# Two projections of a hybrid decoder: value columns taken 512 at a time, and where the deferred pieces stand

## The chip, the cores and the metric

The kernel runs on one core of a Trainium2 chip. The metric is the device time of one launch in microseconds, the median of the runs. TensorE (PE in the profile) multiplies, VectorE (DVE), ScalarE (ACT) and GpSimd (POOL) do the elementwise work, and SyncE (SP) and ScalarE issue the transfers. Each engine works through its own queue in order.

## What is computed

Two layers, 512 tokens, width 1024, 256 memory tokens, all float32. Each layer projects the normed residual to 6664 columns, feeds four groups of heads, multiplies each group by its gate and maps back with one output projection:

```python
def hybrid_layer(x, mem, ...):
    proj = rmsnorm(x, pre_g) @ w_in
    y_ret = retention(ret_q, ret_k, ret_v) * silu(ret_g)          # 4 heads of 128, decay masks
    y_ssd = ssd_mixer(xbc, z, dt_raw, ...)                        # conv, chunked scan, 8 heads of 64
    y_sb = stick_breaking(sb_q, sb_k, sb_v) * silu(sb_g)          # 4 heads of 128
    y_mem = memory_read(mem_q, rmsnorm(mem), w_mem_kv) * silu(mem_g)
    y = concatenate([y_ret, y_ssd, y_sb, y_mem]) @ w_out
    return x + rmsnorm(y, post_g)

def memory_read(q, mem_n, w_mem_kv):
    k, v = split(mem_n @ w_mem_kv, 2)                             # 256 tokens x 512 each
    return softmax(q @ k.T * d ** -0.5) @ v
```

Retention normalises each head's output over its 128 features. The kernel takes the mean out of the values, sums the squares over the features with a matmul against ones, and multiplies the output by the reciprocal root of each token.

## The kernel before

Every operand of a matmul is split into a high part h and a low part l, both float32r, and a product is three matmuls, h h + h l + l h (`mm3`). The residual lies turned, features first, in `hTh` and `hTl`, eight chunks of 128 features (kc).

**Projections.** `proj_b` gives 128 output features for all 512 tokens: the weights are the stationary side, hT the moving one, 8 x 3 matmuls of 512 columns. It is used for queries, keys, gates and the convolution's inputs. `proj_a` gives values with the tokens on the partitions: a slice of hT of 128 tokens is stationary and 256 columns of weights move. It takes the feature chunks in two halves of four, and in each half goes over the token chunks (four, two for the memory). So 512 value columns need two calls; two token chunks share a bank of 512 columns. The stick-breaking values (`sb_v`) call it with 8 columns more for dt, and once without. The retention values (`ret_v`) call it twice, the memory values (`mem_v`) once for each half of the columns.

**Weights.** They come from memory in blocks of 1 MB (`raw`, two buffers), each cut in two half-blocks. A half-block of 128 x 1024 is split by one cast on ScalarE (L286, to `wh`) and one subtraction on VectorE (L287, to `wl`). There are five buffers of wh and wl; `w_take` hands out the next half-block, and `w_prefetch` writes the splits that follow, five half-blocks ahead. A split waits until the buffer's earlier matmuls are over.

**Values.** `ret_v` subtracts each head's mean (reduction L681, scaling L686) and splits the result into pairs. `mem_v2` scales by the memory's norm and splits.

**Order.** The program counts units: each `proj_b` is one (`tick`), each `proj_a` two. Work that has to wait is put off with `defer(n, f)` and runs n units later. For a retention head, `ret_head2` multiplies scores by values and squares them on two half-partitions (L743, L744, L746, L747), `ret_head3` runs a one-row matmul of ones and those squares (`onesr`), and `row_rstd` makes the reciprocal root: a copy of the row (L707), a DMA to 32 partitions (L709), GpSimd's add and power (L710, L711), a DMA to memory (L713) and one that broadcasts it to 128 partitions (L715). `scaled` (L757) multiplies the head's output by it, five units after. Each retention head is three units: q, k and a gate of the memory group. After the heads come the two SSD groups, with convolution (L808, L810, L813) and gates (L821, L953).

The framework's scheduler sets the final order of each engine's queue, from the dependences and its own estimate of times; the start (`start`) alone is written out by hand. Tiles come from pools: `s` (33 buffers of 512 columns), `y` (16), `r` (9), and eight PSUM banks, four `pj` for projections and four `mx` for the rest.

Of the kernel before, what the change touches and what calls it, by code (L numbers as in the profile page):

```python
# [78 lines left out]
def pack_weights(w_in, w_mem_kv, w_out):  # L79

    src = {"w_in": w_in, "w_mem_kv": w_mem_kv, "w_out": w_out}
    out = []
    for l in range(DEPTH):
        for kind, name, spec in BLOCKS:
            w = src[name][l]
            o = []
            for s in range(2):
                if kind == "b":
                    t = w[:, spec[s]:spec[s] + P].reshape(KC, P, P)
                elif kind == "o":  # L90
                    half, j = spec
                    rows = OUT_ROWS[4 * j + 2 * s:4 * j + 2 * s + 2]
                    t = np.stack([w[r:r + P, 512 * half:512 * half + 512] for r in rows])
                elif kind == "d":
# [73 lines left out]
class Builder:  # L168
# [206 lines left out]
    def proj_a(self, x=None, nt=NT, extra=0, between=(), turns=False):  # L375
# [3 lines left out]
        xh, xl = x or self.hk  # L379
        n = 256 + extra  # L380
# [3 lines left out]
        for s in range(2):  # L384
            for f in between if s else ():
                f()
            w = [self.w_take(nk) for _ in range(4 // nk)]
            if self.starting:
                (wh, wl), out = w[0], banks[0]
                for low in range(2):  # L390
                    for t in range(nt):
                        for j in range(4):
                            o, kc, ts = out[:, n * t:n * t + n], 4 * s + j, slice(P * t, P * t + P)
                            first, last = s + low + t + j == 0, (s, low, t, j) == (1, 1, nt - 1, 3)
                            if low:
                                self.mm(o, xh(kc)[:, ts], wl[:, j], False, last)
                            else:
                                self.mm(o, xh(kc)[:, ts], wh[:, j], first, False)
                                self.mm(o, xl(kc)[:, ts], wh[:, j], False, False)
                continue  # L400
# [8 lines left out]
            self.w_prefetch()  # L409
        return banks  # L410
# [130 lines left out]
    def mem_v(self):  # L541
        self.mem_v2(self.proj_a(self.mx_, 2)[0])

    def mem_v2(self, b):
        nc, p = self.nc, Pair(self, 512, "y")
        for t in range(2):
            s, r = slice(256 * t, 256 * t + 256), self.mcol[:, t:t + 1]
            nc.scalar.activation(p.h[:, s], b[:, s], AF.Copy, scale=r)
            nc.vector.scalar_tensor_tensor(out=p.l[:, s], in0=b[:, s], scalar=r, in1=p.hf[:, s], op0=ALU.mult, op1=ALU.subtract)
        self.mv.append(p)  # L550
# [78 lines left out]
    def sb_head(self, h, v):  # L629
# [3 lines left out]
        w = [t[:, c] for t, c in self.packed([P * (t + 1) for t in range(NT)], self.buf)]  # L633
# [18 lines left out]
        self.defer(3, self.sb_head2, h, v, w, y)  # L652
        return y

    def sb_head2(self, h, v, w, y):
# [7 lines left out]
        self.defer(1, self.sb_head3, h, v, wT, y)  # L663
# [9 lines left out]
    def ret_v(self):  # L673
# [3 lines left out]
        out = [[None, None], [None, None]]  # L677
        for half in range(2):
            for i, b in enumerate(self.proj_a()):
                st = self.tiny(4)  # L680
                nc.vector.tensor_reduce(out=st, in_=v3(b, 4), op=ALU.add, axis=AX.X)  # L681
                nc.vector.tensor_scalar(out=st, in0=st, scalar1=-1.0 / HD, scalar2=None, op0=ALU.mult)
                vt = self.buf()
                for j in range(4):
                    t, h = 2 * i + j // 2, 2 * half + j % 2
                    nc.vector.tensor_scalar(out=vt[:, P * j:P * j + P], in0=b[:, P * j:P * j + P],  # L686
                                            scalar1=st[:, j:j + 1], scalar2=ginv[:, 4 * t + h:4 * t + h + 1],
                                            op0=ALU.add, op1=ALU.mult)
                out[i][half] = self.pair(vt)
# [45 lines left out]
    def ret_head2(self, h, v, sc, y):  # L735
        nc = self.nc
        b = self.mx()
        for c in range(NT):
            self.mm3(b[:, P * c:], *self.vcols(v, c, h), sc[c][0], sc[c][1], c == 0, c == NT - 1)
# [10 lines left out]
    def ret_head3(self, h, z, y):  # L750
# [219 lines left out]
    def out_proj(self, l):  # L970
# [51 lines left out]
        if not last:  # L1022
# [3 lines left out]
            for i in range(2):  # L1026
                self.mem_v()
            self.behind(self.turn[2], self.marks[1])
# [43 lines left out]
    def start(self):  # L1072
# [37 lines left out]
        def v0():  # L1110
            a.append(self.normed_a(xs[2]))
            self.turned(hn[0], 0)
        v = [self.proj_a(self.mx_, 2, between=[v0])[0]]
        self.w_prefetch(7)
        hn.append(self.normed_b(a[2], preB))
        self.turned(hn[1], 1)
        a.append(self.normed_a(xs[3]))
        self.mem_cols()
        self.w_prefetch(8)
        hn.append(self.normed_b(a[3], preB))  # L1120

        def v1():
            self.turned(hn[2], 2)
        v.append(self.proj_a(self.mx_, 2, between=[v1])[0])
# [5 lines left out]
        for i in range(2):  # L1130
            self.mem_v2(v[i])
# [8 lines left out]
    def layer(self, l):  # L1140
        self.exp_ln_phase()
        while len(self.mv) < 2:
            self.mem_v()
# [54 lines left out]
```

## Time and profile before

| | us |
|---|---|
| median of 3 runs (961.93 to 963.8) | 961.94 |
| profiled execution | 961.89 |
| its span | 960.2 |
| TensorE busy | 949.8 |
| VectorE busy | 657.4 |
| ScalarE busy | 456.8 |
| GpSimd busy | 104.4 |

The span is what the trace covers; 1.7 us of the profiled execution lie around it. Durations of matmuls overlap (a matmul of 512 columns is shown with some 390 ns, and the next one starts 227 ns after it), so starts are to be compared. "Idle before" is the time in which an engine had nothing in hand ahead of an instruction, with what ended it.

### The profile page before, as it was taken

To read this page: it belongs to the slowest core of one execution; us is meant where nothing else is said; L and a number is where in the kernel's file an instruction comes from. 1 tells how busy PE (TensorE), PEld (TensorE's weight loads), DVE (VectorE), ACT (ScalarE), POOL (GpSimd) and SP (SyncE) were. 2 spreads that over 40 slices of the span, in tenths; PEclk is the share of its full clock that TensorE was granted. 3 is DMA by queue.
4 is the path that set the end of the run, shared out by engine and by line. 5 is a ranking of instruction groups with operands and counts; after the bars stand their busy time and mean duration, and the time that the engine had idled before them with its cause. 6 is when DMAs were issued, how large, how long until landed. Compare 5 with 4: busy or idle time off the path is not lost.

```text
span 960.2 us, 13253 instructions
## 1 busy us (share of the span) xinstructions
PE 949.8 (99%) x5151; PEld 812.6 (85%) x5151; DVE 657.4 (68%) x1056; ACT 456.8 (48%) x844; POOL 104.4 (11%) x160
## 2 busy tenths in 40 slices
PE   9999999999999999999999999999999999999997
PEld 7998889988887888888899888898888878888885
DVE  5855567767777796854487465768777968877443
ACT  6544566534554342643465345665344543435341
POOL 1100000001231201100040000000003421102001
PEclk9999999999999999999999999999999999999999
DMA  9442212122232524344344222112222333423502
GB/s 347 149 147 80 88 45 88 45 88 88 91 108 99 165 88 121 115 160 142 120 170 184 89 88 71 62 45 88 77 78 85 134 105 116 120 91 120 195 25 87
DMA packets 26734, 105.79 MB, mean 110 GB/s; under 512 B 4144, under 2 KB 4400, under 8 KB 17456
## 3 DMA queue, kind: packets, MB, share of 16 engines
q10 hardware_dynamic: 10224, 73.44, 21.8%
q1 hardware_dynamic: 16448, 31.52, 10.0%
q8 instruction: 40, 0.66, 0.3%
q14 instruction: 22, 0.18, 0.1%
HBM read 100.63 MB, written 4.28 MB: 109 GB/s over the span
## 4 chain that ended last, share of the span: by engine, by line
PE 88%; DVE 5%; DMA 3%; ACT 1%; issue 1%; POOL 1%; DVEq 0%; SPq 0%; ACTq 0%; POOLq 0%
PE pj L278 65%; PE mx L278 22%; DVE s L647 1%; DMA r<-row 1%; PE mx L599 1%; PE mx L449 1%; DMA mem<-memT 1%; DMA s<-acs 1%; DVE wl L287 1%; DMA t<-r 1%; POOL t L711 1%; DVE s L810 1%; DVE s L646 0%; PE mx L661 0%; DVE s L287 0%
## 5 line engine op out<-in xcount | busy, mean ns | idle before, releaser
L278 PE MATMUL pj<-hTh,wh 128*128 128x512 f32 x704 | 277.5, 394 | 0.0
L278 PE MATMUL pj<-hTl,wh 128*128 128x512 f32 x704 | 276.6, 393 | 0.0
L278 PE MATMUL pj<-hTh,wl 128*128 128x512 f32 x704 | 275.4, 391 | 0.0
L287 DVE TENSOR_TENSOR wl<-raw,wh 128x1024 fp32r<-128x1024 f32 (+2 forms) x155 | 183.7, 1190 | 114.2 <-ACT wh L286 107.3
L286 ACT CAST wh<-raw 128x1024 fp32r<-128x1024 f32 (+2 forms) x155 | 158.0, 1025 | 178.9 <-PE pj L278 153.7
L278 PEld LDWEIGHTS pj<-hTh,wl 128*128 128x128 f32 x704 | 132.3, 188 | 26.7
L278 PEld LDWEIGHTS pj<-hTh,wh 128*128 128x128 f32 x704 | 132.3, 188 | 26.4
L278 PEld LDWEIGHTS pj<-hTl,wh 128*128 128x128 f32 x704 | 132.4, 188 | 25.7
L278 PE MATMUL pj<-wh,s 128*128 128x512 f32 (+1 forms) x384 | 99.8, 355 | 0.0
L278 PE MATMUL mx<-s,s 128*128 128x256 f32 (+4 forms) x616 | 97.5, 310 | 0.3
L278 PEld LDWEIGHTS mx<-s,s 128*128 128x128 f32 (+1 forms) x616 | 84.6, 178 | 12.9 <-issue 3.1
L278 PE MATMUL mx<-wh,s 128*128 128x512 f32 x256 | 79.2, 389 | 0.0
L278 PEld LDWEIGHTS pj<-wh,s 128*128 128x128 f32 x384 | 66.1, 189 | 10.5
L730 POOL TENSOR_SCALAR_AFFINE_SELECT s<-s 128x128 fp32r<-128x128 f32 x64 | 21.2, 363 | 420.6 <-DVE s L287 420.6
L278 PE MATMUL pj<-wl,s 128*128 128x512 f32 (+1 forms) x192 | 63.4, 354 | 0.0
L278 PE MATMUL pj<-wh,hTh 128*128 128x256 f32 (+1 forms) x208 | 60.3, 290 | 0.5 <-DVE s L556 0.5
L287 DVE TENSOR_TENSOR s<-mx,s 128x512 fp32r<-128x512 f32 (+2 forms) x86 | 42.1, 517 | 26.0 <-ACT s L286 25.6
L278 PE MATMUL pj<-wl,hTh 128*128 128x256 f32 (+1 forms) x208 | 59.5, 286 | 0.0
L278 PE MATMUL pj<-wh,hTl 128*128 128x256 f32 (+1 forms) x208 | 58.5, 284 | 0.0
L278 PEld LDWEIGHTS mx<-wh,s 128*128 128x128 f32 x256 | 48.1, 188 | 10.0
L286 ACT CAST s<-mx 128x512 fp32r<-128x512 f32 (+2 forms) x86 | 36.7, 456 | 40.1 <-PE mx L278 24.1
L287 DVE TENSOR_TENSOR s<-y,s 128x512 fp32r<-128x512 f32 x64 | 41.3, 688 | 19.7 <-ACT s L286 14.0
(167 smaller groups left out, 1324.5 us busy)
## 6 DMA issues: line engine op xcount, KB each, us to landing
raw<-wts ACTq DMA_DIRECT2D x69, 1024.0 KB, 4.8
s<-x SPq DMA_DIRECT2D x24, 256.0 KB, 3.7
s<-acs SPq DMA_DIRECT2D x16, 256.0 KB, 6.1
raw<-wts SPq DMA_DIRECT2D x3, 1024.0 KB, 8.3
r<-row SPq DMA_DIRECT2D x12, 256.0 KB, 3.9
s<-acs SPq DMA_DIRECT2D x16, 128.0 KB, 6.7
x<-s SPq DMA_DIRECT2D x8, 256.0 KB, 2.0
out<-s SPq DMA_DIRECT2D x8, 256.0 KB, 2.0
```

The costliest lines, as they stand in the source:

```text
L278: return self.nc.tensor.matmul(out, lhsT, rhs, start=start, stop=stop)
L286: self.nc.scalar.copy(h, src)
L287: self.nc.vector.tensor_sub(l, src, hf)
L449: x = self.nc.tensor.transpose(b[:, P * j:P * j + P], hn[i][:, P * j:P * j + P], self.con("ident", P))
L599: nc.tensor.transpose(b[:, P * t:P * t + P], w[t // 2][:, o:o + P], self.con("ident", P))
L647: nc.vector.tensor_tensor_scan(out=u[:, ::-1], data0=u[:, ::-1], data1=u[:, ::-1], initial=0.0, op0=ALU.add, op1=ALU.bypass)
L711: nc.gpsimd.tensor_tensor(out=c, in0=c, in1=self.mhalf[:RP], op=ALU.pow)
L730: nc.gpsimd.affine_select(out=d, in_=d, pattern=[[1, P]], compare_op=ALU.is_ge, fill=0.0, base=0, channel_multiplier=-1)
L810: nc.vector.scalar_tensor_tensor(out=acc[:, s:], in0=b[:, :SEQ - s], scalar=tap(3 - s), in1=acc[:, s:], op0=ALU.mult, op1=ALU.add)
```

## The change

The values of the memory and of the retention are projected by a new function, `proj_v`: 512 columns of weights move at once, and one token chunk follows the other, each through all eight feature chunks into a bank of its own. For that the half-blocks are packed anew (kind "v": 256 features by 512 columns), four of them are taken ahead of the first chunk, and the prefetch of the next four is written behind the last. Each token chunk counts one unit for the retention values and two for the memory values. In the start, where the weights still arrive, it goes half-block by half-block instead, over both token chunks. `proj_a` stays for the stick-breaking values.

```diff
-    b += [("a", "w_mem_kv", GW + 256 * i) for i in range(2)]
+    b += [("v", "w_mem_kv", (GW, 512 * i)) for i in range(2)]
...
-    b += [("a", "w_in", RET_V + 256 * i) for i in range(2)]
+    b += [("v", "w_in", (RET_V, 512 * i)) for i in range(2)]
...
+    def proj_v(self, x=None, nt=NT, between={}):
+        xh, xl = x or self.hk
+        banks = [self.pj() for _ in range(nt)]
+        self.marks = []
+        if self.starting:
...
+        w = [self.w_take(2) for _ in range(4)]
+        for t in range(nt):
+            self.tick(4 // nt)
+            ts = slice(P * t, P * t + P)
+            for kc in range(KC):
+                wh, wl = w[kc // 2]
+                self.mm3(banks[t], xh(kc)[:, ts], xl(kc)[:, ts], wh[:, kc % 2], wl[:, kc % 2], kc == 0, kc == KC - 1)
+                if kc % 2:
+                    self.marks.append(self.last_mm)
+        self.w_prefetch()
+        return banks
```

The tiles of values now hold one token chunk and all heads, so their users take other columns of them:

```diff
+        for t, b in enumerate(banks):
+            p, r = Pair(self, 512, "y"), self.mcol[:, t:t + 1]
+            nc.scalar.activation(p.h, b, AF.Copy, scale=r)
+            nc.vector.scalar_tensor_tensor(out=p.l, in0=b, scalar=r, in1=p.hf, op0=ALU.mult, op1=ALU.subtract)
+            self.mv.append(p)
...
-            o = 256 * m + HD * (h % 2)
-            v = self.mv[h // 2]
+            o, v = HD * h, self.mv[m]
...
+        for t, b in enumerate(self.proj_v()):
+            st = self.tiny(HEADS)
+            nc.vector.tensor_reduce(out=st, in_=v3(b, HEADS), op=ALU.add, axis=AX.X)
+            nc.vector.tensor_scalar(out=st, in0=st, scalar1=-1.0 / HD, scalar2=None, op0=ALU.mult)
+            vt = self.buf(tag="r")
+            for h in range(HEADS):
+                c = slice(HD * h, HD * h + HD)
+                nc.vector.tensor_scalar(out=vt[:, c], in0=b[:, c], scalar1=st[:, h:h + 1],
+                                        scalar2=ginv[:, 4 * t + h:4 * t + h + 1], op0=ALU.add, op1=ALU.mult)
+            out.append(self.pair(vt))
```

The deferred pieces get other distances, the weight tiles of the stick-breaking heads another pool, and `scaled` is pinned to its place in the program's order:

```diff
-        w = [t[:, c] for t, c in self.packed([P * (t + 1) for t in range(NT)], self.buf)]
+        w = [t[:, c] for t, c in self.packed([P * (t + 1) for t in range(NT)], lambda: self.buf(tag="r"))]
...
-        self.defer(3, self.sb_head2, h, v, w, y)
+        self.defer(4, self.sb_head2, h, v, w, y)
...
-        self.defer(1, self.sb_head3, h, v, wT, y)
+        self.defer(2, self.sb_head3, h, v, wT, y)
...
-        self.defer(5, self.scaled, y, self.row_rstd(vb, self.con("reps", HEADS * RJ, RP)[:, RJ * h:RJ * h + RJ]))
+        self.defer(7, self.scaled, y, self.row_rstd(vb, self.con("reps", HEADS * RJ, RP)[:, RJ * h:RJ * h + RJ]))
...
-        self.nc.vector.tensor_mul(y, y, rB)
+        self.tc.keep_in_program_order(self.nc.vector.tensor_mul(y, y, rB))
```

Two places of the queues show what moves. The first is VectorE's queue where the first SSD group begins, in layer 0. Before, the scaling of head 2 (L757) stands ahead of the squares of head 3 (L744, L747):

```order
L810 SCALAR_TENSOR_TENSOR s_3113<-pj_3084,hp_776,s_3113 128x510
L810 SCALAR_TENSOR_TENSOR s_3113<-pj_3084,hp_776,s_3113 128x509
L287 TENSOR_TENSOR wl_3147<-raw_2946,wh_3146 128x1024
L757 TENSOR_TENSOR y_2632<-y_2632,r_2915 128x512
L744 TENSOR_TENSOR r_3008<-r_3008,r_3009 64x512
L813 SCALAR_TENSOR_TENSOR s_3114<-s_3114,s_3113 128x512
L810 SCALAR_TENSOR_TENSOR s_3152<-pj_3121,hp_776,s_3152 128x511
L747 TENSOR_TENSOR r_3013<-r_3008,r_3013 64x512
L810 SCALAR_TENSOR_TENSOR s_3152<-pj_3121,hp_776,s_3152 128x510
L810 SCALAR_TENSOR_TENSOR s_3152<-pj_3121,hp_776,s_3152 128x509
```

After, line numbers are 18 or 19 higher there: L762 and L765 are L744 and L747, L776 is L757, L829 and L832 the convolution, L840 and L972 a gate. The first row is the scaling of head 1, the last that of head 2:

```order
L776 TENSOR_TENSOR y_2298<-y_2298,r_2552 128x512
L829 SCALAR_TENSOR_TENSOR s_3004<-pj_2973,hp_724,s_3004 128x511
L765 TENSOR_TENSOR r_2864<-r_2859,r_2864 64x512
L829 SCALAR_TENSOR_TENSOR s_3004<-pj_2973,hp_724,s_3004 128x510
L290 TENSOR_TENSOR wl_3038<-raw_2896,wh_3037 128x1024
L829 SCALAR_TENSOR_TENSOR s_3004<-pj_2973,hp_724,s_3004 128x509
L832 SCALAR_TENSOR_TENSOR s_3005<-s_3005,s_3004 128x512
L840 SCALAR_TENSOR_TENSOR s_3041<-s_3041,pj_3012 128x512
L972 SCALAR_TENSOR_TENSOR y_1449<-y_1449,s_3041 128x512
L290 TENSOR_TENSOR wl_3073<-raw_2896,wh_3072 128x1024
L840 SCALAR_TENSOR_TENSOR s_3078<-s_3078,pj_3047 128x512
L776 TENSOR_TENSOR y_2484<-y_2484,r_2766 128x512
```

Head 3's L765 now has head 1's scaling ahead of it, and head 2's scaling stands behind it, two weight splits and a gate further on.

The second place is VectorE's queue at the end of the retention values of layer 0. Before, the rows around one weight split (L287 to wl), with the reduction and scalings of the values (L681, L682, L686) and the scans of stick-breaking head 3 (L646, L647, L649):

```order
L681 TENSOR_REDUCE t_2150<-pj_2042 128x4
L646 SCALAR_TENSOR_TENSOR s_1776<-mx_1813,s_1776 128x512
L287 TENSOR_TENSOR s_1829<-mx_1839,s_1828 128x384
L682 TENSOR_SCALAR t_2150<-t_2150 128x4
L647 SCALAR_TENSOR_TENSOR s_1776<-s_1776 128x512
L287 TENSOR_TENSOR s_1831<-mx_1845,s_1830 128x256
L686 TENSOR_SCALAR s_1979<-pj_1868,t_1976,consts 128x128 x4
L649 TENSOR_TENSOR s_1776<-mx_1813,s_1776 128x512
L287 TENSOR_TENSOR s_1829<-mx_1850,s_1828 128x128
L681 TENSOR_REDUCE t_2162<-pj_2043 128x4
L287 TENSOR_TENSOR wl_2147<-raw_1922,wh_2146 128x1024
L287 TENSOR_TENSOR s_1985<-s_1979,s_1984 128x512
```

After (L290 is L287, L699, L700 and L704 are the values, L665, L666 and L668 the scans; pj_1760 to pj_1763 are the four token chunks):

```order
L704 TENSOR_SCALAR r_1979<-pj_1761,t_1976,consts 128x128 x4
L704 TENSOR_SCALAR r_1991<-pj_1762,t_1988,consts 128x128 x4
L290 TENSOR_TENSOR wl_1945<-raw_1479,wh_1944 128x1024
L668 TENSOR_TENSOR r_1709<-mx_1735,r_1709 128x384
L290 TENSOR_TENSOR wl_1951<-raw_1627,wh_1950 128x1024
L665 SCALAR_TENSOR_TENSOR r_1710<-mx_1747,r_1710 128x512
L290 TENSOR_TENSOR wl_1955<-raw_1627,wh_1954 128x1024
L699 TENSOR_REDUCE t_2000<-pj_1763 128x4
L290 TENSOR_TENSOR s_1789<-mx_1794,s_1788 128x512
L290 TENSOR_TENSOR s_1791<-mx_1801,s_1790 128x384
L666 SCALAR_TENSOR_TENSOR r_1710<-r_1710 128x512
L700 TENSOR_SCALAR t_2000<-t_2000 128x4
L290 TENSOR_TENSOR wl_1961<-raw_1948,wh_1960 128x1024
```

Before, one weight split stands among twelve rows, and the next one ahead of it is three rows further up. After, three stand within five rows, a fourth six rows on, and the scalings of three token chunks are ahead of them.

## Rows read from the trace of the kernel before

**Rows 1.** The page's first table: busy time, share of span and instructions of each engine
```profile
PE 949.8 (99%) x5151; PEld 812.6 (85%) x5151; DVE 657.4 (68%) x1056; ACT 456.8 (48%) x844; POOL 104.4 (11%) x160
```

**Rows 2.** The page's chain of work that ended last, shares by engine
```profile
PE 88%; DVE 5%; DMA 3%; ACT 1%; issue 1%; POOL 1%; DVEq 0%; SPq 0%; ACTq 0%; POOLq 0%
```

**Rows 3.** The same chain in order of time: start, us, engine, tile, line, count
```profile
398.68 40.59 PE pj L278 x179
439.26 38.08 PE mx L278 x168
...
483.16 7.07 PE pj L278 x59
...
505.56 5.79 PE pj L278 x48
...
520.99 9.00 PE pj L278 x75
```

**Rows 4.** Groups of PE's instructions by line and shape: count | busy us, mean ns
```profile
L278 PE MATMUL pj<-wh,hTh 128*128 128x256 f32 x192 | 55.8, 291 | 0.5 <-DVE s L556 0.5
L278 PE MATMUL pj<-wl,hTh 128*128 128x256 f32 x192 | 54.9, 286 | 0.0
L278 PE MATMUL pj<-wh,hTl 128*128 128x256 f32 x192 | 53.9, 284 | 0.0
...
L278 PE MATMUL pj<-wh,s 128*128 128x256 f32 x128 | 20.6, 286 | 0.0
...
L278 PE MATMUL pj<-wl,s 128*128 128x256 f32 x64 | 13.6, 284 | 0.0
```

**Rows 5.** What PE waited for: us in total, times, longest us
```profile
PE mx L278 <- DVE r L747: 1.8, 2, 0.9
...
PE pj L278 <- DVE s L556: 0.5, 2, 0.2
```

**Rows 6.** PE in order of time at two one-row matmuls: start, us, instruction [idle before]
```profile
307.41 0.39 PE L278 MATMUL pj<-hTl,wh 128*128 128x512 f32 x1
308.69 0.39 PE L278 MATMUL mx<-r,onesr 128*1 128x512 f32 x1 [0.89 <-DVE r L747]
...
778.34 0.39 PE L278 MATMUL pj<-hTl,wh 128*128 128x512 f32 x1
779.64 0.39 PE L278 MATMUL mx<-r,onesr 128*1 128x512 f32 x1 [0.91 <-DVE r L747]
```

**Rows 7.** DVE in order of time ahead of the first of them
```profile
298.72 1.23 DVE L287 TENSOR_TENSOR wl<-raw,wh 128x1024 fp32r<-128x1024 f32 x1
305.37 0.69 DVE L757 TENSOR_TENSOR y<-y,r 128x512 f32<-128x512 f32 x1 [5.42 <-DMA r<-row]
305.98 0.68 DVE L744 TENSOR_TENSOR r<-r,r 64x512 f32<-64x512 f32 x1
306.58 0.68 DVE L813 SCALAR_TENSOR_TENSOR s<-s,s 128x512 f32<-128x512 f32 x1
307.18 0.73 DVE L810 SCALAR_TENSOR_TENSOR s<-pj,hp,s 128x511 f32<-128x511 f32 x1
307.95 0.69 DVE L747 TENSOR_TENSOR r<-r,r 64x512 fp32r<-64x512 f32 x1
```

**Rows 8.** The chain ahead of L757, and all waits of L757 (us, times)
```profile
292.95 2.96 DMA t<-r
296.53 2.91 POOL t L711
300.94 4.41 DMA r<-row
...
  DMA r<-row: 20.2, 6
```

**Rows 9.** Groups of DVE's and ACT's instructions by line and shape, columns as in rows 4
```profile
L287 DVE TENSOR_TENSOR wl<-raw,wh 128x1024 fp32r<-128x1024 f32 x145 | 177.1, 1224 | 110.9 <-ACT wh L286 104.2 <-PE mx L278 6.2
...
L686 DVE TENSOR_SCALAR s<-pj,t,consts 128x128 f32<-128x128 f32 x32 | 10.9, 408 | 0.0
...
L681 DVE TENSOR_REDUCE t<-pj 128x4 f32<-128x512 f32 x8 | 5.5, 688 | 0.5 <-PE pj L278 0.5
...
L286 ACT CAST wh<-raw 128x1024 fp32r<-128x1024 f32 x145 | 152.1, 1052 | 169.5 <-PE pj L278 148.0 <-PE mx L278 16.0 <-DVE wl L287 2.9
```

**Rows 10.** Stretch of layer 0's retention values: length, busy us of each engine, granted clock
```profile
150.00:184.00 34.00, 33.65 (x266) 31.91 (x266) 25.01 (x47) 21.84 (x50) 0.00 (x0) 1.00 0.18 63
```

More of the change, by code (lines that the diff above doesn't have):

```diff
@@ L93, in pack_weights @@
                     t = np.stack([w[r:r + P, 512 * half:512 * half + 512] for r in rows])
+                elif kind == "v":
+                    rows = slice(spec[1] + 256 * s, spec[1] + 256 * s + 256)
+                    t = w[rows, spec[0]:spec[0] + 512].reshape(2, P, 512)
                 elif kind == "d":
@@ L373, in proj_b, with proj_a @@
         return out
-    def proj_a(self, x=None, nt=NT, extra=0, between=(), turns=False):
+    def proj_a(self, extra=0, turns=False):
         self.tick(2)
-        xh, xl = x or self.hk
-        n = 256 + extra
+        xh, xl = self.hk
+        nt, n = NT, 256 + extra
         per, nk = (1, 2) if extra else (2, 4)
@@ L384, in proj_a @@
         for s in range(2):
-            for f in between if s else ():
-                f()
             w = [self.w_take(nk) for _ in range(4 // nk)]
[L388 to L400, printed above, removed]
             for t in range(nt):
@@ L409, in proj_a @@
             self.w_prefetch()
+        return banks
[4 more added lines that the diff above has]
+        if self.starting:
+            for s in range(4):
+                for f in between.get(s, ()):
+                    f()
+                wh, wl = self.w_take(2)
+                for low in range(2):
+                    for t in range(nt):
+                        for j in range(2):
+                            kc, ts = 2 * s + j, slice(P * t, P * t + P)
+                            if low:
+                                self.mm(banks[t], xh(kc)[:, ts], wl[:, j], False, (s, j) == (3, 1))
+                            else:
+                                self.mm(banks[t], xh(kc)[:, ts], wh[:, j], s + j == 0, False)
+                                self.mm(banks[t], xl(kc)[:, ts], wh[:, j], False, False)
+            return banks
+        w = [self.w_take(2) for _ in range(4)]
+        for t in range(nt):
+            self.tick(4 // nt)
[6 more added lines that the diff above has]
+        self.w_prefetch()
         return banks
@@ L541, in mem_v, with mem_v2 @@
     def mem_v(self):
[L542 to L550, printed above, removed]
+        self.mem_v2(self.proj_v(self.mx_, 2))
+    def mem_v2(self, banks):
+        nc = self.nc
+        for t, b in enumerate(banks):
[3 more added lines that the diff above has]
+            self.mv.append(p)
     def scaled_pair(self, b, scale):
@@ L676, in ret_v @@
         ginv = self.con("ginv", 16)
[L677 to L689, printed above, removed]
+        out = []
+        for t, b in enumerate(self.proj_v()):
[8 more added lines that the diff above has]
+            out.append(self.pair(vt))
         return out
@@ L738, in ret_head2 @@
         for c in range(NT):
-            self.mm3(b[:, P * c:], *self.vcols(v, c, h), sc[c][0], sc[c][1], c == 0, c == NT - 1)
+            o = slice(HD * h, HD * h + HD)
+            self.mm3(b[:, P * c:], v[c].h[:, o], v[c].l[:, o], sc[c][0], sc[c][1], c == 0, c == NT - 1)
         nc.scalar.copy(y, b)
@@ L1025, in out_proj @@
                 self.behind(self.turn[i], self.last_mm)
-            for i in range(2):
-                self.mem_v()
-            self.behind(self.turn[2], self.marks[1])
+            self.mem_v()
+            self.behind(self.turn[2], self.marks[5])
     def load_x(self, t):
@@ L1108, in start, with v1, v2, v3 @@
         hn.append(self.normed_b(a[1], preB))
-        def v0():
+        def v1():
             a.append(self.normed_a(xs[2]))
             self.turned(hn[0], 0)
[L1113 to L1122, printed above, removed]
+        def v2():
+            self.w_prefetch(7)
+            hn.append(self.normed_b(a[2], preB))
+            self.turned(hn[1], 1)
+            a.append(self.normed_a(xs[3]))
+            self.mem_cols()
+            self.w_prefetch(8)
+            hn.append(self.normed_b(a[3], preB))
+        def v3():
             self.turned(hn[2], 2)
-        v.append(self.proj_a(self.mx_, 2, between=[v1])[0])
+        v = self.proj_v(self.mx_, 2, {1: [v1], 2: [v2], 3: [v3]})
         row = self.to_rows(self.mcol, 2)
@@ L1129, in start @@
         self.w_load(5)
-        for i in range(2):
-            self.mem_v2(v[i])
+        self.mem_v2(v)
         self.w_prefetch(12)
```

2 lines of the change are left out of this document (removed).

## The prediction

> **What bounds the kernel now.** I read the page's engine table first: TensorE is busy in 99% of the span, VectorE in 68%, ScalarE in 48% [rows 1]. The chain of work that ended last says the same: 88% of it is TensorE, 5% VectorE, 3% DMA [rows 2]. So a change pays by what it takes out of TensorE's queue, or out of the few places where that queue stands still. Busy time can't tell how dense the queue is, since the matmuls overlap; the spacing of their starts can. The chain in order of time gives it: 179 matmuls of 512 columns take 40.59 us, 168 take 38.08 us, both 226.7 ns each; with 256 columns 59 take 7.07, 48 take 5.79 and 75 take 9.00 us, 119.8 to 120.6 ns each [rows 3]. Two matmuls of 256 columns thus cost 13 ns more than one of 512: half the columns is not half the time. Last I read where TensorE waits by the list of waits: 1.8 us in two places for VectorE's L747, 0.5 us in two for L556 [rows 5]; the rest of its waits lie ahead of the first projection and stay.
>
> **Part 1, wider matmuls.** Per layer the memory values took 2 halves x 8 k-chunks x 2 token chunks x 3 = 96 matmuls of 256 columns and now take 48 of 512; the retention values took 192 and now take 96. Over two layers 576 narrow ones become 288 wide ones. The groups by shape bear the count out: the three groups from hT to a 256-column pj hold 3 x 192, of which a third are the stick-breaking values' second half, which stays (384 left); the memory values are the 128 + 64 that read s [rows 4]. Every one lies on TensorE's queue, which is the path, so the gain is 288 x (2 x 120.0 - 226.7) = 288 x 13.3 ns = **3.8 us**. Bounds: with 119.8 ns 3.7 us, with 120.6 ns 4.2 us; if the 48 pairs of the start give nothing, because the start's splits set the pace there, 3.2 us.
>
> At both widths the rows leave some 13 ns beside the columns: 226.7 = 213.3 + 13.4 and 120.0 = 106.7 + 13.3, columns at 2.4 GHz, with a granted clock of 1.00 [rows 3, 10]. The Trainium skill (TensorE: Matmul & The Clock Gate, Back-to-back issue gap) gives the gap of a warm matmul as N / 2.4 plus 2.5 ns: by it, an estimate, a pair would save 2.5 ns and this part 0.7 us. The trace does not agree: that formula has 109 ns for 256 columns where the rows have 120.
>
> **Part 2, the scaling of the retention heads.** In both layers TensorE stands at the one-row matmul of the last head's variance: it starts 1.28 us after the matmul ahead of it in layer 0 and 1.30 us in layer 1, where 0.23 is usual [rows 6]. VectorE's rows show why. It ends a weight split at 299.95, then stands 5.42 us at L757, the scaling of head 2 by its broadcast row, until a DMA lands; L744, L813 and L810 follow, and only then L747, which the matmul needs [rows 7]. VectorE works in order, so L757's wait is paid by all behind it. The DMA could not be earlier: copy to 32 partitions, GpSimd's add and power, write to memory, broadcast back, 292.95 to 305.35 in the chain [rows 8]. L757 waited so six times, 20.2 us in all [rows 8]; two of them reach TensorE.
>
> The change asks for seven units instead of five and keeps the instruction where the program has it. The order shows it: head 2's scaling leaves its place ahead of L744 and stands behind the next head's L765 (the former L747), a z gate and two weight splits; what stands ahead of L765 now is head 1's scaling, whose data is a whole head older. A head is three units, 3 x 24 x 0.227 = 16.3 us, more than the 12.4 us of the chain. So these waits go, and with them 1.05 us in each layer: **2.1 us**. What is late next there is nothing VectorE does: without 5.42 us of standing its L747 ends over 4 us ahead of the matmul. Bounds: 0, if another wait takes its place, and 2.1.
>
> **Part 3, the weights of a wide block.** Four half-blocks are taken at once, of five buffers, and the next four are split only as the last token chunk releases them. Each costs 1.05 us of ScalarE and 1.22 us of VectorE [rows 9], as before, but they come in a bunch: in VectorE's order three stand within five rows, where there was one in thirteen. The first is needed by retention head 0's k projection. Its buffer is free after 6 of the last chunk's 24 matmuls; the remaining 18 and the 24 of the q projection, whose weights are split already, take 42 x 0.227 = 9.5 us, against 2.3 us for cast and subtraction. VectorE's queue is the tighter bound: from the end of chunk 2 it has the reduction (0.69), twelve scalings of 128 columns (12 x 0.41 = 4.9) [rows 9], and some 3.5 us of head 3's scans ahead of that split: 10.3 us with it, against 10.9 us of two projections and about 1.7 us of head 3's logits on TensorE. The margin is some 2 us by durations and 3 by the shorter steps at which VectorE starts one instruction after another. VectorE is busy 25.01 us of 34 in this stretch [rows 10], so I take **0**, and keep 0 to 2 us per layer for the range.
>
> **Part 4, the rest.** The value tiles' arithmetic is the same (four scalings of 128 columns and a reduction for each of four tiles), only dealt out chunk by chunk. For the memory values eight scalings of 256 columns on VectorE and eight on ScalarE become four wide ones on each, off the path. The weight tiles of the stick-breaking heads and the new value tiles move to the nine r buffers: three for each head, and a tile comes round three heads later, when its transposes, four units behind, have run. Of the four pj banks each has the three other chunks or projections between its last matmul and its next use. The 0.24 us at the first matmul of the retention values in each layer [rows 5] may go or come back as another wait: 0, with 0.5 us of gain for the range. The bytes that are moved stay the same.
>
> **Sum.** The profiled execution took 961.89 us with a span of 960.2; the median of the runs is 961.94. 961.9 - 3.8 - 2.1 = **956.0 us**.
>
> **Rivals.**
> (a) A new wait takes the old one's place at each layer, one of about 1 us, from the bunched splits or behind a moved piece: 956.0 + 2.1 = 958.1. For it: the margins of part 3 are of 2 to 3 us and rest on an order. Against: VectorE loses 20.2 us of standing.
> (b) The 13 ns are no cost of each matmul but of its operands, and the wide block, which takes a new stationary slice of hT for every matmul and has w as the moving side, shows twice as much: then the pair saves nothing and 961.9 - 2.1 = 959.8 is left. Against it: the 168 + 179 wide matmuls of rows 3 are of that very kind, y slices stationary and w_out moving, at 226.7 ns. The Trainium skill's formula (TensorE: Matmul & The Clock Gate, Back-to-back issue gap), by itself, would end at 959.1.
> (c) The scheduler's order holds more slack than I count: the 0.5 us of L556 and one or two of the small gaps go too, and part 1 gives 4.2: 961.9 - 4.2 - 2.1 - 0.5 = 955.1.
> (d) Slower: the bunched splits come so late that TensorE stands at k of retention head 0 in each layer. It decides once VectorE is more than the 3 us of margin behind; to lose the 5.9 us gained and 2 more, it must be 7 us behind in both layers, TensorE waiting 4 us in each: 964. A wait for an r buffer ahead of the split could do it, since everything on VectorE queues behind. Against: in the trace of before the same stage has 9 us to spare on VectorE per layer [rows 10].
> (e) Between (a) and (d): waits of 2 to 3 us in each layer, 960 to 962, no difference.
>
> **Chances.** Forecast 0.55, (a) 0.16, (b) 0.06, (c) 0.10, (d) 0.05, (e) 0.08. A difference of 0.2%, 1.9 us, is about what a measurement of this kernel can tell; faster is below 960.0. The forecast, (a), (c) and half of (b), which ends at that line, are faster: 0.84; half of (b) and (e) are the same: 0.11; (d) is slower: 0.05. The range goes from below (c), with 1.3 us for small gaps that I can't assign, to (b): 953.8 to 959.9. It leaves out (d) and (e).
>
> **What would show it.** Right: 288 fewer matmuls; at 512 columns in the value blocks a spacing of 227 ns; no wait of TensorE for the variance's subtraction; VectorE's scaling without idle time ahead of it. Wrong: TensorE waiting for wl or wh in the first projections behind a value block; VectorE standing at the r tiles; a spacing above 235 ns in the wide blocks, which would eat part 1 whole (288 x 13 ns is lost at 240).

## The result and the profile after

The changed kernel takes 954.56 us (median of 6 runs, 953.91 to 955.93) against 961.93 us before: a ratio of 0.9923, 95% interval 0.991 to 0.9936. That is 7.4 us less, where the prediction had 5.9. The profiled execution took 954.77 us with a span of 953.0; the one before had 960.2.

The page of the changed kernel, its engine table and the shares of its chain of work that ended last, beside [rows 1, 2]:

```profile
PE 944.9 (99%) x4863; PEld 797.0 (84%) x4863; DVE 654.5 (69%) x1052; ACT 455.5 (48%) x840; POOL 102.0 (11%) x160
...
PE 98%; DMA 1%; DVEq 0%; SPq 0%; ACT 0%; issue 0%; POOLq 0%; POOL 0%; ACTq 0%; DVE 0%
```

There are 288 matmuls fewer, as counted. TensorE's share of the chain went from 88 to 98%; VectorE's 5% and two of the 3% of DMA are gone. What is left of TensorE's waits lies in the start (waits of PE: us in total, times, longest):

```profile
PE mx L281 <- POOL b L193: 1.2, 1, 1.2
PE pj L281 <- ACT s L512: 0.6, 1, 0.6
```

Neither the wait for the variance's subtraction nor the one for L556 is there any more [rows 5]. VectorE in order of time, where [rows 7] showed it standing 5.42 us (L762, L776 and L765 are the former L744, L757 and L747):

```profile
298.15 0.68 DVE L762 TENSOR_TENSOR r<-r,r 64x512 f32<-64x512 f32 x1
298.75 0.68 DVE L832 SCALAR_TENSOR_TENSOR s<-s,s 128x512 f32<-128x512 f32 x1
299.35 0.68 DVE L776 TENSOR_TENSOR y<-y,r 128x512 f32<-128x512 f32 x1
299.95 0.73 DVE L829 SCALAR_TENSOR_TENSOR s<-pj,hp,s 128x511 f32<-128x511 f32 x1
300.72 0.69 DVE L765 TENSOR_TENSOR r<-r,r 64x512 fp32r<-64x512 f32 x1
```

The scaling that now stands there, head 1's, has no idle time ahead of it, and none of the eight scalings waits any more, where six did [rows 8]. TensorE in order of time, at the matmul that needs L765:

```profile
305.88 0.39 PE L281 MATMUL pj<-hTh,wh 128*128 128x512 f32 x1
306.11 0.40 PE L281 MATMUL mx<-r,onesr 128*1 128x512 f32 x1
```

It starts 0.23 us behind its neighbour, 4.7 us after L765 ends; [rows 6] had 1.28.

### The profile page after: what moved, and what is told of

It reads as the page before. It is cut to its first block, busy times and chain, and to the rows that moved or that the text cites. A ratio compares the mean times of both kernels' runs of the same rounds, so it can differ in the third digit from the quotient of the medians.

```text
span 953.0 us, 12669 instructions
## 1 busy us (share of the span) xinstructions
PE 944.9 (99%) x4863; PEld 797.0 (84%) x4863; DVE 654.5 (69%) x1052; ACT 455.5 (48%) x840; POOL 102.0 (11%) x160
## 4 chain that ended last, share of the span: by engine, by line
PE 98%; DMA 1%; DVEq 0%; SPq 0%; ACT 0%; issue 0%; POOLq 0%; POOL 0%; ACTq 0%; DVE 0%
PE pj L281 72%; PE mx L281 23%; PE mx L680 1%; DMA mem<-memT 1%; PE mx L619 1%; PE mx L469 1%; PE mx L890 0%; PE mx L910 0%; DVEq L1210 0%; POOLq L1210 0%; ACT s L1058 0%; ACT s L512 0%; SPq L495 0%; SPq L343 0%; SPq L1094 0%
## 5 line engine op out<-in xcount | busy, mean ns | idle before, releaser
L290 DVE TENSOR_TENSOR wl<-raw,wh 128x1024 fp32r<-128x1024 f32 (+2 forms) x155 | 183.7, 1190 | 123.3 <-ACT wh L289 119.3
L281 PE MATMUL pj<-wh,s 128*128 128x512 f32 x320 | 97.7, 391 | 0.0
L281 PE MATMUL mx<-s,s 128*128 128x128 f32 (+4 forms) x616 | 94.8, 309 | 0.0
L281 PEld LDWEIGHTS pj<-wh,s 128*128 128x128 f32 x320 | 59.7, 188 | 12.5
L747 POOL TENSOR_SCALAR_AFFINE_SELECT s<-s 128x128 fp32r<-128x128 f32 x64 | 20.5, 354 | 395.0 <-DVE s L290 395.0
L290 DVE TENSOR_TENSOR s<-mx,s 128x512 fp32r<-128x512 f32 (+2 forms) x86 | 41.8, 515 | 27.8 <-ACT s L289 27.8
L281 PE MATMUL pj<-wl,s 128*128 128x512 f32 x160 | 60.2, 390 | 0.0
L290 DVE TENSOR_TENSOR s<-y,s 128x512 fp32r<-128x512 f32 x64 | 41.2, 686 | 19.7 <-ACT s L289 14.0
L289 ACT CAST s<-y 128x512 fp32r<-128x512 f32 x64 | 36.5, 617 | 29.4 <-PE mx L281 22.0
L281 PE MATMUL mx<-wl,s 128*128 128x512 f32 x128 | 49.6, 389 | 0.0
L281 PE MATMUL pj<-wl,hTh 128*128 128x256 f32 (+2 forms) x144 | 48.7, 338 | 0.0
```

Of the source, the lines that this page charges most:

```text
L281: return self.nc.tensor.matmul(out, lhsT, rhs, start=start, stop=stop)
L289: self.nc.scalar.copy(h, src)
L290: self.nc.vector.tensor_sub(l, src, hf)
L747: nc.gpsimd.affine_select(out=d, in_=d, pattern=[[1, P]], compare_op=ALU.is_ge, fill=0.0, base=0, channel_multiplier=-1)
```

## The experiments

Three theories were to be told apart. The prediction's: the gain is the width (3.8 us) and the scaling (2.1 us), and the distances and homes are worth nothing. A first rival: the spread of the deferred pieces is a gain of its own. A second: the distances and homes are no gain, but the price of the wide block, without which it would lose more than it saves. All ratios are to the kernel before, run on the same chip in the same call; the first row is its median in the calls of the experiments (962.3 to 962.5; 961.9 in that of the changed kernel).

| kernel | value columns | distances | homes (weights, values) | scaling | us | ratio, 95% interval |
|---|---|---|---|---|---|---|
| before | 256 | 3, 1 | s, s | 5, free | 962.3 | |
| scaled_alone | 256 | 3, 1 | s, s | 7, pinned | 959.46 | 0.9969 (0.9957 to 0.998) |
| spread_only | 256 | 4, 2 | r, r | 7, pinned | 957.34 | 0.9946 (0.9934 to 0.9959) |
| narrow_pairs | 2 x 256, chunk by chunk | 4, 2 | r, r | 7, pinned | 957.48 | 0.9952 (0.9939 to 0.9964) |
| changed kernel | 512 | 4, 2 | r, r | 7, pinned | 954.56 | 0.9923 (0.991 to 0.9936) |
| pin_five | 512 | 4, 2 | r, r | 5, pinned | 954.75 | 0.9922 (0.9908 to 0.9935) |
| home_w_back | 512 | 4, 2 | s, r | 7, pinned | 954.71 | 0.9926 (0.9913 to 0.9938) |
| split_twice | 512, a split more | 4, 2 | r, r | 7, pinned | 957.35 | 0.9946 (0.9933 to 0.9959) |
| scaled_back | 512 | 4, 2 | r, r | 5, free | 959.50 | 0.9967 (0.9955 to 0.9979) |
| distances_back | 512 | 3, 1 | r, r | 7, pinned | 962.88 | 1.0007 (0.9996 to 1.0018) |
| value_home_only | 512 | 3, 1 | s, r | 7, pinned | 963.16 | 1.0001 (0.9991 to 1.0012) |
| homes_back | 512 | 4, 2 | s, s | 7, pinned | 968.66 | 1.0067 (1.0055 to 1.008) |
| home_v_back | 512 | 4, 2 | r, s | 7, pinned | 968.78 | 1.0066 (1.0053 to 1.0078) |
| wide_alone | 512 | 3, 1 | s, s | 5, free | 977.75 | 1.016 (1.0146 to 1.0174) |

### The scaling: alone, taken back, and pinned at five units

The kernel before, with

```diff
-        self.defer(5, self.scaled, y, self.row_rstd(vb, self.con("reps", HEADS * RJ, RP)[:, RJ * h:RJ * h + RJ]))
+        self.defer(7, self.scaled, y, self.row_rstd(vb, self.con("reps", HEADS * RJ, RP)[:, RJ * h:RJ * h + RJ]))
...
-        self.nc.vector.tensor_mul(y, y, rB)
+        self.tc.keep_in_program_order(self.nc.vector.tensor_mul(y, y, rB))
```

> The kernel before, with one part of the change alone: the scaling of a retention head stands seven units behind instead of five and is pinned to its place. Theory: VectorE's standing at the scaling held up TensorE, the 2.1 us at the variance's ones (1.05 us in each layer) and also the 0.17, 0.21 and 0.15 us ahead of matmuls of the SSD groups that are gone in the changed kernel (0.54 us in all): 961.9 - 2.1 - 0.5 = 959.3 us. Rival 1: only the two long waits are its doing, the small ones go with the wide blocks: 959.8. Rival 2: another wait takes the place (case a of the prediction): 961 to 962.

It took 959.46 us, 2.9 us less. Waits of PE in scaled_alone:

```profile
PE pj L278 <- ACT s L492: 1.3, 1, 1.3
PE mx L278 <- POOL b L190: 1.2, 1, 1.2
PE pj L278 <- DVE s L556: 0.5, 2, 0.2
```

The wait for L747 is gone. So are three smaller delays of TensorE in the SSD groups (0.17 us at 311.7, 0.21 at 782.6 and 0.15 at 811.5 us in the kernel before), which the prediction had left among the small gaps: with 2.1 they make 2.6 us. VectorE's standing had reached TensorE in five places, not in two. The wait for L556 stays, so it belongs to another part.

The changed kernel with the same two lines turned back:

> The changed kernel with the scaling of the retention heads as before: five units, not pinned. Theory: the two waits of TensorE at the variance's ones come back, 2.1 us, and the three small ones of the SSD groups with them, 0.5 us: 954.6 + 2.6 = 957.2 us. Rival 1: only the two long ones come back: 956.7. Rival 2: the spread of the other pieces had removed them already: 954.6.

It took 959.50 us, 4.9 more than the changed kernel, and more than the 2.9 that the part gives alone. VectorE in order of time in scaled_back:

```profile
296.32 1.23 DVE L290 TENSOR_TENSOR wl<-raw,wh 128x1024 fp32r<-128x1024 f32 x1 [0.20 <-ACT wh L289]
304.51 0.69 DVE L776 TENSOR_TENSOR y<-y,r 128x512 f32<-128x512 f32 x1 [6.96 <-DMA r<-row]
...
307.09 0.69 DVE L765 TENSOR_TENSOR r<-r,r 64x512 fp32r<-64x512 f32 x1
```

The same stand as in [rows 7], 6.96 us long. TensorE, in order of time:

```profile
305.01 0.39 PE L281 MATMUL pj<-hTl,wh 128*128 128x512 f32 x1
307.83 0.40 PE L281 MATMUL mx<-r,onesr 128*1 128x512 f32 x1 [2.43 <-DVE r L765]
...
309.42 0.63 PE L281 MATMUL pj<-hTl,wh 128*128 128x512 f32 x1
309.84 0.63 PE L281 MATMUL pj<-hTh,wl 128*128 128x512 f32 x1
310.27 0.63 PE L281 MATMUL pj<-hTh,wh 128*128 128x512 f32 x1
```

The row lands 0.9 us earlier than before (304.5 against 305.4), but TensorE arrives 2.4 us earlier (305.0 against 307.4), since the width and the spread have shortened its work up to there. So it waits longer: the one-row matmul is 2.6 us late instead of 1.05. Behind this wait the matmuls start 0.42 us apart instead of 0.23, eight of them, 1.6 us more. The windows show the clock there (length, busy us of PE, PEld, DVE, ACT, POOL, then PEclk, DMA share and GB/s):

```profile
305.00:309.00 4.00, 1.57 (x8) 0.95 (x7) 3.90 (x7) 1.57 (x2) 0.00 (x0) 1.00 0.00 0
309.00:312.40 3.40, 3.40 (x10) 2.63 (x8) 3.37 (x6) 2.97 (x5) 0.00 (x0) 0.50 0.01 3
```

The granted clock falls to 0.50, the lower of the two levels, for 3.4 us behind the wait. In layer 1 the matmul is 1.2 us late and the clock stays. 2.6 + 1.6 + 1.2 = 5.4 us, against 5.2 between the two spans.

The changed kernel with seven turned back to five, and the pin kept:

> The changed kernel with the scaling pinned to its place, but five units after its row is sent for, as before. Theory: the pin is what counts, since without it the framework's scheduler puts the scaling at the same early place for five units and for seven; at five the scaling of each head still stands behind the next head's squares, and its data has had a head's time: 954.6 us, no wait of TensorE for the variance's squares. Rival: at five it stands waiting for its row again: 957 to 959.5, as in the kernel with the old scaling.

954.75 us, the same as the changed kernel, and no wait of TensorE for the squares. Beside the pin the distance of seven does nothing; the pin is what keeps the scaling behind the next head's L765. Seven units without the pin were not run.

### The width, by itself

In the changed kernel every matmul of a value block is done as two halves, in the order that it has (in the start likewise):

```diff
...
-                self.mm3(banks[t], xh(kc)[:, ts], xl(kc)[:, ts], wh[:, kc % 2], wl[:, kc % 2], kc == 0, kc == KC - 1)
+                for o in range(2):
+                    c = slice(256 * o, 256 * o + 256)
+                    self.mm3(banks[t][:, c], xh(kc)[:, ts], xl(kc)[:, ts], wh[:, kc % 2, c], wl[:, kc % 2, c],
+                             kc + o == 0, (kc, o) == (KC - 1, 1))
```

> The changed kernel, its order and tiles as they are, with each of the 288 matmuls of 512 columns in the value blocks done as two of 256. It measures the price of the width by itself. Theory: 288 x 13.3 ns = 3.8 us more, 954.6 + 3.8 = 958.4 us, or 3.2 us if the 48 of the start are paced by the start's splits. Rival: a pair saves 2.5 ns: 955.3.

957.48 us: the width is worth 2.9 us by the medians, less than either end of the prediction's part 1. The two intervals, of some 1.2 us to either side, would leave room for its 3.2 us; what speaks for the smaller price are the rows of the matmuls themselves. The chain in order of time of narrow_pairs, inside the value blocks (start, us, count):

```profile
154.25 2.69 PE pj L281 x22
...
173.57 3.23 PE pj L281 x27
```

and of the changed kernel:

```profile
154.98 5.74 PE pj L281 x25
...
173.86 3.92 PE pj L281 x17
```

A matmul of 256 columns takes 119.6 to 122.3 ns here, as in [rows 3], but one of 512 takes 229.6 to 230.6, not the 226.7 of the output projection's unbroken rows. A pair thus saves some 10 ns and not 13.3; 288 x 10 = 2.9 us. The trace of before had this price too, where projections are cut by transposes; its chain has retention head 0's first 19 matmuls of 512 columns at 229.5 ns each:

```profile
185.31 4.36 PE pj L278 x19
```

The Trainium skill (TensorE: Matmul & The Clock Gate, Back-to-back issue gap) would have 2.5 ns for the pair by its formula, which it gives for an isolated matmul; four times that was measured, so the formula does not hold for these streams.

### The spread without the wide blocks

The kernel before with the distances 4 and 2, weight and value tiles in the r buffers, and the pinned scaling, but with its 256-column blocks (the changes of these lines are those of the diff above):

> The kernel before, with its 256-column value blocks, and everything of the change but the wide blocks: the distances 4 and 2, the homes, the pinned scaling at seven. Theory: with two half-blocks, each with banks that are free at its end, the distances only take the two small waits at the retention values away (0.55 us in each layer) on top of the pinned scaling's 2.9 us: 959.5 - 1.1 = 958.4 us. Rival: the distances are worth something only beside the wide block, 959.5, or they make a new wait here, 960 to 962.

957.34 us: 2.1 us less than scaled_alone, of which 1.1 are the two small waits at the retention values in each layer (0.28 and 0.28 us), which are gone. The rest is not accounted for: of the 2.4 us between the two profiled spans, 0.9 lie ahead of layer 0's first projection of 512 columns, where the program is the same. So the spread is a gain of its own, of 1.1 to 2.1 us, in the old blocks too, and there it costs nothing; how it divides between distances and homes was not tested there. It also says the width again: 957.34 - 954.56 = 2.8 us.

### The wide blocks without the spread

The changed kernel with distances, homes and scaling as before, which leaves the wide blocks alone:

> The changed kernel with only its wide value blocks: the deferred pieces have their old distances (3, 1 and 5), the scaling isn't pinned, the tiles have their old homes. Theory: 288 pairs of 256-column matmuls become 288 of 512, 13.3 ns each, 3.8 us, and the waits of the scaling (2.1 us and 0.5 us) and those at the value block (0.55 us in each layer) stay: 961.9 - 3.8 = 958.1 us. Rival 1: the small waits at the value block go with the new order of the block itself: 957.0. Rival 2: the pair saves 2.5 ns, 0.7 us: 961.2.

977.75 us: not 3.8 us faster than before but 15.4 slower. Waits of PE in wide_alone:

```profile
PE mx L680 <- DVE s L290: 9.0, 4, 3.5
PE mx L281 <- DVE s L290: 2.5, 2, 1.3
```

TensorE stands at the transposes of the stick-breaking heads (L680) and behind them. In three stretches of the span, 13.3 us in all, the granted clock is 0.50. To find which of the spread's parts matters, each was taken back by itself. First the homes:

```diff
-        w = [t[:, c] for t, c in self.packed([P * (t + 1) for t in range(NT)], lambda: self.buf(tag="r"))]
+        w = [t[:, c] for t, c in self.packed([P * (t + 1) for t in range(NT)], self.buf)]
...
-            vt = self.buf(tag="r")
+            vt = self.buf()
```

> The changed kernel with the weight tiles of the stick-breaking heads and the value tiles back in the s buffers. Theory of the prediction: the homes are worth nothing, 954.6 us. Rival, from the sum of the runs so far: the wide blocks with all old pieces took 977.8, the old distances cost 8.3 us and the old scaling 4.9, and 10 us are left over, which would be the homes: 964 to 965, with TensorE waiting at transposes.

968.66 us, 14 more than the changed kernel: the homes, which the prediction costed at nothing, are worth more than the width and the scaling together. Then each of the two lines alone:

> The changed kernel with the weight tiles of the stick-breaking heads back in the s buffers; the value tiles stay in the r buffers. Theory: with both homes back the kernel took 968.7, because a value tile in the s buffers comes free late, so VectorE's scalings out of the four value banks stand late, the next projection finds no bank, and TensorE has only stick-breaking pieces left, which wait. With the value tiles in the r buffers, which the weight tiles now leave free, each bank is scaled right behind its sums: no wait of TensorE, 954 to 955 us, the same as the changed kernel. Rival: it is the home of the weight tiles that counts: 960 or more.

> The changed kernel with the four value tiles back in the s buffers; the weight tiles of the stick-breaking heads stay in the r buffers. Theory: this edit alone brings the late scalings back, and with them TensorE's waits at transposes between the value block and the first projection behind it: 964 to 969 us. Rival: the nine tiles that the weights leave free in the s buffers are enough for the values: 954.6.

954.71 and 968.78 us: it is the value tiles' home, and only that. VectorE's sum and scalings of the first value chunk and the scalings of the third in home_w_back, where TensorE waits in the start alone:

```profile
153.43 0.69 DVE L699 TENSOR_REDUCE t<-pj 128x4 f32<-128x512 f32 x1 [2.16 <-PE pj L281]
...
154.36 1.37 DVE L704 TENSOR_SCALAR r<-pj,t,consts 128x128 f32<-128x128 f32 x4
...
168.89 1.36 DVE L704 TENSOR_SCALAR r<-pj,t,consts 128x128 f32<-128x128 f32 x4
```

and the first chunk's in home_v_back, with the value tiles in s:

```profile
156.70 0.67 DVE L699 TENSOR_REDUCE t<-pj 128x4 f32<-128x512 f32 x1
...
189.87 1.36 DVE L704 TENSOR_SCALAR s<-pj,t,consts 128x128 f32<-128x128 f32 x4
```

The first sum comes 3 us later there, the scalings of that chunk 35 us later. Until then all four pj banks hold values, and the next projection has none. The changed kernel itself lies between the two. Its first sum starts at 156.6 us, its scalings come in a bunch of twelve:

```profile
174.39 1.04 DVE L704 TENSOR_SCALAR r<-pj,t,consts 128x128 f32<-128x128 f32 x3
175.34 0.95 DVE L666 TENSOR_TENSOR_SCAN r<-r 128x384 f32<-128x384 f32 x1
176.21 2.94 DVE L704 TENSOR_SCALAR r<-pj,t,consts 128x128 f32<-128x128 f32 x9
```

The fourth of them, which empties the first bank, ends some 2.3 us before the next projection needs a bank, at 178.9. So there is no wait, but the margin is small. TensorE in home_v_back:

```profile
182.82 0.30 PE L680 MATMUL mx<-consts,r 128*128 128x128 f32 x1 [3.50 <-DVE t L700]
183.36 2.96 PE L281 MATMUL mx<-s,s 128*128 128x512 f32 x12 [0.24 <-DVE s L290]
186.11 2.04 PE L680 MATMUL mx<-consts,r 128*128 128x128 f32 x10
189.02 4.04 PE L281 MATMUL mx<-s,s 128*128 128x512 f32 x24 [0.86 <-DVE s L290]
192.89 0.45 PE L281 MATMUL pj<-hTh,wh 128*128 128x512 f32 x1
```

Retention head 0's first projection starts at 192.9, where the changed kernel has it at 178.9. In between only stick-breaking pieces are left, three of which wait for a step of VectorE, 4.6 us in all, and no projection stands between to cover that. Part of the price is the clock (columns as in the windows above):

```profile
184.30:187.70 3.40, 3.40 (x17) 3.40 (x17) 1.17 (x2) 1.14 (x3) 0.00 (x0) 0.50 0.22 92
```

Behind the wait of 3.5 us the granted clock is at the lower level for 3.4 us, in layer 1 too (658.8 to 662.1). At the full clock that work would take half as long, so, as an estimate, some 3.4 of the 13.4 us between this span and the changed kernel's are the clock. The Trainium skill (Perfetto Trace Analysis, Optimizing Tensor Performance, Matmuls) asks that independent groups rotate through the PSUM banks, so that one bank is emptied under the next group's matmuls. The trace agrees: the wide block takes all four banks of the projections in one go, and pays 14 us, waits and clock together, where they are emptied late. The old block, of two banks at a time, had the old homes and no such wait [rows 5]. Which earlier tile the value tile waits for in s was not traced. Nor was the chunk-by-chunk block run with halves of 256 columns and the old home, so that the four banks, and not the width, make the home matter is read from the traces alone.

Then the distances:

```diff
-        self.defer(4, self.sb_head2, h, v, w, y)
+        self.defer(3, self.sb_head2, h, v, w, y)
...
-        self.defer(2, self.sb_head3, h, v, wT, y)
+        self.defer(1, self.sb_head3, h, v, wT, y)
```

> The changed kernel with the two later pieces of a stick-breaking head at their old distances, 3 and 1 units instead of 4 and 2. Theory: the two small waits of TensorE at the value block, 0.28 us at its first matmul and 0.28 us behind the transposes in each layer, came from these pieces standing in a bunch ahead of the block, and come back: 954.6 + 1.1 = 955.7 us. Rival: they went because the block now goes chunk by chunk: 954.6.

962.88 us, 8.3 more, and not 1.1. Both sides of the expectation missed. Waits of PE in distances_back:

```profile
PE pj L281 <- DVE s L715: 4.1, 2, 2.1
PE pj L281 <- DVE r L704: 1.5, 2, 0.7
```

The small waits at the value block did not come back. In their place TensorE waits in each layer for a bank that the values' scaling (L704) empties late, 0.7 us, and 40 us later for one that a retention head's rotation (L715) empties late, 2.1 us. The profiled execution is one of the fastest of this kernel, at 961.1 us; the last section comes back to that. The last run of this group takes the weight tiles out of the r buffers too, so that the values need not wait for them:

> The changed kernel with the old distances (3 and 1) and the weight tiles back in the s buffers: of the spread, only the value tiles' new home and the pinned scaling are left. Theory: the old distances cost 8.3 us because the value tiles then waited for r buffers that the weight tiles held; with those out of the r buffers the scalings stand right behind the sums, and the distances are worth only the small waits: 955 to 957 us. Rival: the distances cost what they cost, whatever the homes: 962 to 963.

963.16 us: the theory falls by half. The wait for L704 is gone, and the small wait at the value block's first matmul is back (0.24 us in each layer, for L576, the former L556), but the one for L715 stays, 1.8 us in each layer, and the time with it. VectorE stands there 3.2 us at the splits of the scores, for ScalarE's casts, ahead of the rotation; the changed kernel has the same stand, 3.9 us, but it ends at 214.2 us and not at 219.6. Why the shorter distances put it later was not settled.

### The margin of the bunched weight splits

In the changed kernel the first split behind the retention values is subtracted twice:

```diff
                 self.split(x, h[:, c], l[:, c], h[:, c].bitcast(F32))
+                for _ in range(self.again):
+                    self.nc.vector.tensor_sub(l[:, c], x, h[:, c].bitcast(F32))
+                self.again = 0
...
+        self.again = 1 if nt == NT else 0
         self.w_prefetch()
```

> The changed kernel with the first weight split behind the retention values subtracted twice on VectorE; the second subtraction, of 1.2 us, stands a few rows later, behind the next two splits, and TensorE needs it. It tests the margin of the prediction's part 3. In the changed kernel that split ends at 180.3 us in layer 0 and the projection that needs it starts at 184.4, 4 us later. Theory: the second subtraction ends at about 186.5, so TensorE stands some 2 us in each layer: 958 to 960 us. Rival: the order has more slack and nothing moves: 954.6.

957.35 us, 2.8 more, a little under the expectation and for another reason. The second subtraction ends at 186.5 us, as expected, but the scheduler, which plans with it, puts the gate's projection ahead of k's, and nobody waits there. The later k then leads to a wait at the same L715 (waits of PE in split_twice):

```profile
PE pj L281 <- DVE s L720: 1.9, 2, 0.9
```

(L720 is L715 in this kernel.) It is late by 1.1 us in each layer; another 0.4 us lie in the start. So one more subtraction on VectorE is enough to reach TensorE, but not at the place that part 3 of the prediction watched. In the changed kernel itself the margin there is 4.0 us, by the end of the split on VectorE

```profile
179.07 1.21 DVE L290 TENSOR_TENSOR wl<-raw,wh 128x1024 fp32r<-128x1024 f32 x1
```

and the start of k's first matmul on TensorE:

```profile
184.32 0.39 PE L281 MATMUL pj<-hTh,wh 128*128 128x512 f32 x1
```

## Why the prediction came out right, and where it didn't

The time lies in the range, 1.4 us below the forecast, nearest to case (c). But the sum was put together from terms of other sizes. That the two terms of the forecast come to 5.7 us together, where it had 5.9, is luck: the first was 1.0 too large and the second 0.8 too small. The 1.4 us on top are about what the spread gives, which the forecast had at 0.

**Part 1** counted right and priced wrong. The step that failed is the price of a wide matmul: it was taken from [rows 3], where 168 and 179 run unbroken, and carried to blocks where transposes and scores cut them into groups of 1 to 25. There one takes 229 to 231 ns. The part gave 2.8 to 2.9 us and not 3.8, below its bounds of 3.2 to 4.2. No wide matmul stood at the place itself before, but a like place was there to read: the 19 of retention head 0, at 229.5 ns. The narrow matmuls hardly show the effect (119.6 to 122.3 ns cut, 119.8 to 120.6 in [rows 3]), so the error is on the wide side of the difference.

**Part 2** had the mechanism and the place, and was too small: 2.9 us and not 2.1. The list of waits names what TensorE waited for, and two waits named L747; the three smaller delays in the SSD groups went with the same standing and were not followed back to it. That the distance of seven takes part was an error, though a harmless one: the pin alone does it.

**Part 3** held: 0, with a margin of 4.0 us instead of 2 to 3.

**Part 4** is where the reasoning fell while its number stood. Its 0 stands in that nothing is lost in the changed kernel, and is a little low, since the spread gave 1.1 to 2.1 us where up to 0.5 was allowed for. But the sentence that each pj bank "has the three other chunks or projections between its last matmul and its next use" looked at the distance in matmuls and not at what empties the bank. A bank comes free when VectorE has scaled it into a value tile, so it hangs on that tile's buffer. Without the new home the wide blocks cost 14 us, without the distances 8.3; with neither, and with the old scaling, the kernel is 15.4 us slower than before. These two edits are the price of the wide block, and they were priced as bystanders.

**Rivals.** (b) is out by narrow_pairs. (a), (d) and (e) did not happen in the whole kernel, but (d) was close by: with one line less (home_v_back) the kernel would have been slower, at 968.8, further than the 964 that it was given, and by the banks rather than by the late splits.

By parts, taken one on top of the other: scaling 2.9 us (scaled_alone), spread 2.1 (spread_only), width 2.8, in sum 7.8 from 962.3, the kernel before in those calls; in its own call the changed kernel is 7.4 us faster.

## What to carry to other kernels

A block that takes all banks of a pool at once turns whatever empties those banks into part of the matmul's path: look up what each emptying step writes to, and when that tile's buffer comes free, before the step is called hidden. Edits that look like housekeeping (a tile's pool, a distance) may be what pays for the visible one, so cost them by taking them away, not by what they do. A price per instruction is to be read in a stretch that is cut the way the changed stretch will be.

## What the runs showed of the hardware

A wait of TensorE can cost more than its length. Behind the 2.4 us of idle time in scaled_back the granted clock was 0.50 for 3.4 us, and eight matmuls of 512 columns took 0.42 us each: 1.6 us on top of the wait. In home_v_back the same comes behind 3.5 us, in both layers. In homes_back it comes behind a wait of 1.8 us between transposes, and lasts from 180.9 to 187.6 us, with another wait of 0.7 us inside; so too in layer 1. Behind the 0.9 us of [rows 6] and the 2.1 us of the profiled distances_back nothing of the kind is seen. So the length of a wait alone does not say whether the clock falls. The runs of distances_back, with waits of 0.7 and 2.1 us, spread by more than those of most others (those of value_home_only do so too, 959.7 to 965.2 us): two at 961.0 to 961.1 us with a mean granted clock of 0.998, five at 962.8 to 963.0 with 0.996 to 0.997, three at 964.2 to 964.7 with 0.995 and one at 965.6 with 0.993. The profiled one was of the first two. That in the others a wait was followed by the low clock, once or more often, fits the steps of some 1.7 us, but no profile of such a run is there to show it.
